# One core: work buffers at multiples of 512 bytes, and three turnings moved to VectorE in squares of 32x32

## The chip, the cores and the metric

The kernel runs on one core of one Trainium2 chip. A core has five engines beside its 16 DMA engines: TensorE for matrix products, VectorE and ScalarE for work on tiles in the on-chip memory (SBUF), GpSimd, and SyncE, which here issues transfers. The metric is the device time of one execution in microseconds; the median of the runs shown is compared. The profile is that of one execution.

## The reference

The reference is one inference step of a two-layer encoder on two requests that share weights: 1024 prompt rows and 32 sample rows of 1024 features, in float32. Cut to what matters:

```python
for i in range(2):
    mod = silu(c) @ w_ada[i] + b_ada[i]                 # c: one vector per request
    sh1, sc1, gt1, sh2, sc2, gt2 = split(mod, 6)
    h = rmsnorm(x, g_norm[i, 0]) * (1 + sc1) + sh1
    if i == 0:    # spatial gating: h @ w_in (1024 -> 4096), gelu, u and v
        v = rmsnorm(v, g_v)
        s = w_s @ v + b_s      # per group, within chunks of 128 rows (sample: 32 rows)
        mix = (u * s) @ w_out  # 2048 -> 1024
    else:         # means over the last 2, 4, 8, 16 rows minus the row, times w_grp
        mix = pool_mixer(h)
    x = x + gt1 * rmsnorm(mix, g_norm[i, 1])
    h = rmsnorm(x, g_norm[i, 2]) * (1 + sc2) + sh2
    f = square(relu(h @ w_up[i])) @ w_down[i]           # 1024 -> 4096 -> 1024
    x = x + gt2 * rmsnorm(f, g_norm[i, 3])
```

The outputs are x of prompt and sample after both layers, and the states of the mixers.

## The kernel before

Activations are kept turned, features on the 128 partitions and rows of x as columns, in three column tiles: 384, 384 and 288 (256 prompt and the 32 sample rows). `acc[t]` holds tile t's x and sums, as 8 blocks of features by 16 columns of halo and the tile's columns. Each large product is three products in float32r, the fast form of float32 on TensorE: value and weight are split into a high and a low part, and high x high (L902), low x high (L903) and high x low (L904) add up in PSUM. `hh`, `hl` are the parts of the normalised input, `fh`, `fl` (and `ush`, `usl`) those of the hidden values. Their names in PSUM are pf (up), pg (down), pu (into the gating mixer), po (out of it); pv is the v half, where the activations stand in the array and 512 columns of weights stream (L929 to L931).

Weights come from memory in pieces of 512 KB. SyncE issues them (`issue`) in the order of one list, `stream`, into three `raw` slots or, for some, into slots of the weight pool itself. `do_w` lets ScalarE make the high part (L417) and VectorE the low part (L79, the helper that every VectorE operation of this kind has as its line); 16 slots "W" hold them. The same list holds the pieces of `w_ada` for the conditioning. `weave` runs between the product groups: it takes steps of the stream while VectorE has room by a running estimate of both engines' time (`time`), and pulls `fillers`, generators for residuals, modulation, pooling and output. `defer` puts a step off by an estimated time. A tile scheduler turns this into one order for each engine.

The conditioning has two forms. The first 16 pieces are products on TensorE with `csil32` (L457); each result is copied by ScalarE, turned by two TensorE transposes (L474) and summed by VectorE. The other slices are multiplied and summed on VectorE into `aa`, 128 partial sums per value. For each slice `fold` puts four products with the matrix `pick` on TensorE (L521), which add over the partitions into four bands of PSUM; ScalarE copies, TensorE turns (L539), and `ada_finish` adds the bias and makes `mod` and `coef`.

In the gating mixer `gate` multiplies v by the spatial weights: psp by chunks of 128 columns (L1211), and for the sample 32 rows by 32 columns (L1219). At the end of layer 1, x of tile 2 ahead of its last residual is turned by 24 TensorE transposes (L1369), copied by ScalarE and sent through memory (`xtd`), and comes back as `xlast` when the last pass starts (`scale_last`, L1342). In that pass the down products of tile 2 are turned as they come (`turn_last`, L1353), their squares are summed over the features by six small products (L1571), and VectorE adds them, scaled, to `xlast`; six transfers write the result (L1599). The outputs of tiles 0 and 1 are fillers (`to_out`): 48 TensorE transposes (L1615), ScalarE copies into a raw slot, six transfers of 512 KB (L1617).

All buffers come from pools that lay them out in the order of allocation. Before the change the pool `work` starts behind constants whose sizes leave its buffers 32 bytes past a multiple of 64; `acc`, `ident` and `ones` lie at multiples of 64.

Of the kernel before, what the change touches and what calls it, by code (L numbers as in the profile page):

```python
# [9 lines left out]
F32 = mybir.dt.float32  # L10
# [5 lines left out]
P = 128  # L16
# [8 lines left out]
NV = 2  # L25
# [9 lines left out]
def tile_stream_encoder_step(  # L35
# [55 lines left out]
    work = pool("work")  # L91
    psum = pool("psum", space=bass.MemoryType.PSUM)
# [8 lines left out]
    hl = [None] * NT  # L101
    acc = [const.tile([P, KB, HALO + n], F32, name=f"acc{t}") for t, n in enumerate(ncol)]
# [4 lines left out]
    xtd = dram.tile([P, len(LAST), D], F32, name="xtd")  # L107
# [9 lines left out]
    pick = const.tile([P, 36], F32, name="pick")  # L117
    nc.vector.memset(pick, 0.0)
    nc.vector.memset(pick[:, 3:4], 1.0)
    inv = const.tile([P, 16], F32, name="inv")  # L120
    epsT = const.tile([P, 1], F32, name="eps")
# [27 lines left out]
    def t_st(name):  # L149
        return work.tile([P, 4], F32, tag="st", bufs=6, name=name)  # L150

    def t_x(name, shape):
        return work.tile(shape, F32, tag="x3", bufs=3, name=name)

    def t_raw(name):
# [3 lines left out]
    rows = [  # L159
        [(g_norm.rearrange("l f (k p) -> (l f k) p", p=P), 64)],  # L160
        [(b_ada.rearrange("l (k p) -> (l k) p", p=P), 96)],
        [
            (c_prompt.rearrange("o (k p) -> (o k) p", p=P), 8),
            (c_sample.rearrange("o (k p) -> (o k) p", p=P), 8),
            (pool_scale.rearrange("o (k p) -> (o k) p", p=P), 8),
            (sgu_g_v.rearrange("o (k p) -> (o k) p", p=P), 16),
        ],
    ]
    vec_rows = [t_m(f"row{i}") for i in range(3)]
    vecs = [  # L170
        const.tile([P, sum(k for _, k in parts)], F32, name=f"vec{i}")
        for i, parts in enumerate(rows)
    ]

# [6 lines left out]
    csil = const.tile([P, KB, NV], F32, name="csil")  # L181
# [30 lines left out]
    ssx = const.tile([P, 9], F32, name="ssx")  # L212
    nc.vector.memset(ssx, 1.0)
    mod = const.tile([P, 2, 48, NV], F32, name="mod")
    coef = const.tile([P, 2, 4, NV, 8], F32, name="coef")
# [213 lines left out]
    def ada_finish(l, sl, view):  # L429

        nk = 2 * view.shape[1]
        m = mod[:, l, 2 * sl : 2 * sl + nk, :].rearrange("p (s h) v -> p s h v", h=2)
        b = bT[:, l * 48 + 2 * sl : l * 48 + 2 * sl + nk].rearrange("p (s h) -> p s h", h=2)
        tt(out=m, in0=view, in1=b.unsqueeze(3).broadcast_to([P, nk // 2, 2, NV]), op=ALU.add)
        which, k0 = sl // 4, 2 * (sl % 4)
        slot = {1: (0, 0), 2: (1, 1), 4: (2, 2), 5: (3, 3)}.get(which)
        if slot is not None:
            cf, gi = slot
            for v in range(NV):
                stt(  # L440
                    out=coef[:, l, cf, v, k0 : k0 + nk],
                    in0=mod[:, l, 2 * sl : 2 * sl + nk, v],
                    scalar=1.0 if cf in (0, 2) else 0.0,
                    in1=g_of(l, gi)[:, k0 : k0 + nk],
                    op0=ALU.add,
                    op1=ALU.mult,
                )


    pe_folds = []  # L450

    def do_ada_pe(l, sl, q, r):
# [16 lines left out]
        act(out=s[:, :256], in_=pa[:, :256], func=AF.Copy)  # L469

        def fold():
            pb = ps_ms(f"adat{l}_{sl}")
            for h in range(2):
                nc.tensor.transpose(pb[:, h * P : (h + 1) * P], s[:, h * P : (h + 1) * P], ident)  # L474
            red = t_st(f"adar{l}_{sl}")
            nc.vector.tensor_reduce(
                out=red.rearrange("p (h m) -> p h m", h=2),
                in_=pb[:, :256].rearrange("p (h c m) -> p h m c", h=2, c=4)[:, :, 0:NV, :],
                op=ALU.add,
# [1189 lines left out]
```

## Time and profile before

| | |
|---|---|
| median of three runs | 2206.67 us (2204.75 to 2207.15) |
| span of the profiled execution | 2201.9 us; its own time is that and some 4.8 us around it, if it stands at the median |
| TensorE busy | 2178.7 us, 99% |
| VectorE busy | 1376.8 us, 63% |
| ScalarE busy | 986.7 us, 45% |
| GpSimd busy | 0.7 us |
| mean granted TensorE clock | 0.999 |
| DMA | 354,976 packets, 312.98 MB, 142 GB/s |

How to read it: the span is the time from the first instruction to the last. PE is TensorE, PEld its weight loads, DVE VectorE, ACT ScalarE, POOL GpSimd, SP SyncE. A row of a group gives line, engine, operation, output and inputs, shape and count, then busy time and mean ns, then idle time ahead of them. A row of the order in time gives start, duration and the instruction; matmuls overlap, so their pace is the distance of the starts and not the duration. A count of records can be twice that of instructions: a float32 product that isn't float32r has two records.

### The profile page before, as it was taken

To read this page: it belongs to the slowest core of one execution; us is meant where nothing else is said; L and a number is where in the kernel's file an instruction comes from. 1 tells how busy PE (TensorE), PEld (TensorE's weight loads), DVE (VectorE), ACT (ScalarE), POOL (GpSimd) and SP (SyncE) were. 2 spreads that over 40 slices of the span, in tenths; PEclk is the share of its full clock that TensorE was granted. 3 is DMA by queue.
4 is the path that set the end of the run, shared out by engine and by line. 5 is a ranking of instruction groups with operands and counts; after the bars stand their busy time and mean duration, and the time that the engine had idled before them with its cause. 6 is when DMAs were issued, how large, how long until landed. Compare 5 with 4: busy or idle time off the path is not lost.

```text
span 2201.9 us, 33431 instructions
## 1 busy us (share of the span) xinstructions
PE 2178.7 (99%) x13383; PEld 2096.0 (95%) x13383; DVE 1376.8 (63%) x2433; ACT 986.7 (45%) x1679; POOL 0.7 (0%) x6
## 2 busy tenths in 40 slices
PE   7999999999999999999999999999999999999998
PEld 5777899999999999999999999999999999999998
DVE  5665746566869556575747879879675553523375
ACT  4633422134447552323445566656564542313354
POOL 0000000000000000000000000000000000000000
PEclk9999999999999999999999999999999999999999
DMA  8475624243527443343645465555454552302343
GB/s 296 128 250 165 201 81 135 89 143 113 154 82 222 148 145 124 102 131 122 191 125 153 149 182 177 180 185 159 139 171 143 155 153 66 107 10 77 97 121 111
DMA packets 354976, 312.98 MB, mean 142 GB/s; under 512 B 10818, under 2 KB 316682, under 8 KB 354820
## 3 DMA queue, kind: packets, MB, share of 16 engines
q1 hardware_dynamic: 352676, 309.43, 45.3%
q8 instruction: 105, 1.72, 0.3%
q10 hardware_dynamic: 2144, 1.41, 0.2%
q14 instruction: 51, 0.42, 0.1%
HBM read 278.95 MB, written 31.84 MB: 141 GB/s over the span
## 4 chain that ended last, share of the span: by engine, by line
PE 96%; DMA 2%; DVE 1%; ACT 1%; SPq 0%; issue 0%; ACTq 0%; DVEq 0%
PE pf L902 12%; PE pf L904 11%; PE pg L902 11%; PE pg L904 11%; PE pg L903 11%; PE pf L903 11%; PE pu L902 3%; PE pu L904 3%; PE po L902 3%; PE po L904 3%; PE po L903 3%; PE pu L903 3%; PE pv L929 2%; PE pv L930 2%; PE pv L931 2%; PE psp L1211 1%
## 5 line engine op out<-in xcount | busy, mean ns | idle before, releaser
L902 PE MATMUL pf<-hh,wh_up 128*128 128x384 f32 (+1 forms) x1536 | 502.6, 327 | 0.0
L902 PE MATMUL pg<-fh,wh_dn 128*128 128x384 f32 (+1 forms) x1536 | 498.0, 324 | 0.0
L904 PE MATMUL pf<-hh,wl_up 128*128 128x384 f32 (+1 forms) x1536 | 496.5, 323 | 0.0
L904 PE MATMUL pg<-fh,wl_dn 128*128 128x384 f32 (+1 forms) x1536 | 494.8, 322 | 0.0
L903 PE MATMUL pg<-fl,wh_dn 128*128 128x384 f32 (+1 forms) x1536 | 494.6, 322 | 0.0
L903 PE MATMUL pf<-hl,wh_up 128*128 128x384 f32 (+1 forms) x1536 | 490.5, 319 | 0.0
L902 PEld LDWEIGHTS pg<-fh,wh_dn 128*128 128x128 f32 x1536 | 288.8, 188 | 4.4 <-issue 3.3
L79 DVE TENSOR_TENSOR wl_up<-raw,wh_up 128x1024 fp32r<-128x1024 f32 x152 | 185.9, 1223 | 167.8 <-ACT wh_up L417 167.8
L902 PEld LDWEIGHTS pf<-hh,wh_up 128*128 128x128 f32 x1536 | 288.2, 188 | 1.3 <-issue 0.8
L903 PEld LDWEIGHTS pg<-fl,wh_dn 128*128 128x128 f32 x1536 | 288.6, 188 | 0.7
L903 PEld LDWEIGHTS pf<-hl,wh_up 128*128 128x128 f32 x1536 | 288.6, 188 | 0.4
L904 PEld LDWEIGHTS pg<-fh,wl_dn 128*128 128x128 f32 x1536 | 288.5, 188 | 0.0
L904 PEld LDWEIGHTS pf<-hh,wl_up 128*128 128x128 f32 x1536 | 287.9, 187 | 0.0
L417 ACT ACTIVATE wh_up<-raw 128x1024 fp32r<-128x1024 f32 x152 | 161.1, 1060 | 278.6 <-PE pf L903 214.3
L79 DVE TENSOR_TENSOR acc<-acc,pg 128x384 f32<-128x384 f32 (+1 forms) x336 | 173.9, 518 | 165.7 <-PE pg L904 164.4
L417 ACT ACTIVATE wh_dn<-raw 128x1024 fp32r<-128x1024 f32 x152 | 161.0, 1060 | 217.7 <-PE pg L903 180.4
L79 DVE TENSOR_TENSOR wl_dn<-raw,wh_dn 128x1024 fp32r<-128x1024 f32 x152 | 185.9, 1223 | 85.3 <-ACT wh_dn L417 85.1
L79 DVE SCALAR_TENSOR_TENSOR aa<-raw,csil,aa 128x512 f32<-128x512 f32 (+1 forms) x364 | 204.3, 621 | 1.9 <-DMA raw<-in_w_ada_dram 1.5
L1293 ACT ACTIVATE r<-pf 128x384 f32<-128x384 f32 (+1 forms) x192 | 86.8, 452 | 197.1 <-PE pf L904 191.7
L79 DVE TENSOR_TENSOR fl<-r,fh 128x384 fp32r<-128x384 f32 (+1 forms) x192 | 100.3, 522 | 104.6 <-ACT fh L1121 103.4
L902 PE MATMUL pu<-hh,wh_u 128*128 128x384 f32 (+1 forms) x384 | 128.0, 333 | 0.0
L902 PE MATMUL po<-ush,wh_o 128*128 128x384 f32 (+1 forms) x384 | 124.2, 324 | 0.0
(264 smaller groups left out, 2899.6 us busy)
## 6 DMA issues: line engine op xcount, KB each, us to landing
raw<-in_ffn_w_up_dram SPq DMA_DIRECT2D x152, 512.0 KB, 4.1
raw<-in_ffn_w_down_dram SPq DMA_DIRECT2D x152, 512.0 KB, 3.4
raw<-in_w_ada_dram SPq DMA_DIRECT2D x96, 512.0 KB, 3.9
raw<-in_sgu_w_in_dram SPq DMA_DIRECT2D x40, 512.0 KB, 4.6
xd<-acc SPq DMA_DIRECT2D x8, 1536.0 KB, 7.4
raw<-in_sgu_w_out_dram SPq DMA_DIRECT2D x24, 512.0 KB, 4.1
xo_r<-xd SPq DMA_DIRECT2D x32, 384.0 KB, 3.3
vd<-vt SPq DMA_DIRECT2D x32, 256.0 KB, 3.3
```

Source lines behind the costliest of these rows:

```text
L79: return op(out, *args, **kw)
L417: act(out=wh, in_=r, func=AF.Copy)
L902: mm(ps[:, :n], wh, rh, start=i == 0, stop=False)
L903: mm(ps[:, :n], wh, rl, start=False, stop=False)
L904: mm(ps[:, :n], wl, rh, start=False, stop=i == last)
L929: mm(ps[:m, :], a_h, wh[:, o : o + 512], start=k == 0, stop=False)
L930: mm(ps[:m, :], a_h, wl[:, o : o + 512], start=False, stop=False)
L931: mm(ps[:m, :], a_l, wh[:, o : o + 512], start=False, stop=k == KB - 1)
L1211: mm(sp[:, c * P : (c + 1) * P], vl[:, c, k * P : (k + 1) * P], wr[:, c * P : (c + 1) * P], start=True, stop=True,)
L1293: act(out=r[:, :n], in_=ps[:, :n], func=AF.Relu)
```

## The change

It has five parts.

1. A new pool `small` takes small tiles and what isn't a multiple of 512 bytes. With the rest reordered, `acc` and every work buffer (`hh`, `hl`, `fh`, `fl`, the weight and raw slots and so on) start at multiples of 512 bytes.
2. The first conditioning results are turned by VectorE in squares of 32x32 straight from PSUM, and `gather`, four small products with `squares` (four unit matrices of 32 on top of one another), adds the bands. It takes the place of a ScalarE copy and two TensorE transposes each.
3. The other slices are turned by VectorE in squares into the raw slot of the last piece and reduced to `sums`; one `gather` for a whole conditioning vector, ten in all, takes the place of 26 folds and 17 transposes. `ada_finish` writes `shift` or `coef` and no longer both.
4. The sample's spatial product has 128 rows: `vl` is zeroed by GpSimd and `wr` by VectorE ahead.
5. The last x of tile 2 goes to memory unturned (four transfers to `xsd`), comes back in nine transfers that order the squares, and is turned by three VectorE transposes at d = 3, 4, 5. The outputs of tiles 0 and 1 are turned by 16 VectorE transposes of 384 columns into `turned` and written by 64 transfers that put the squares in their places, in runs of 128 bytes, 48 issued by SyncE and 16 by GpSimd. In SyncE's order the last piece of weights stands behind the 24 of tile 0, and the six last output transfers behind the 24 of tile 1. In VectorE's order the first of the three transposes of the last x stands before the accumulation of d = 2, the other two behind that of d = 7.

```diff
@@ -89,6 +89,7 @@
 
     const = pool("const")
     work = pool("work")
+    small = pool("small")
     psum = pool("psum", space=bass.MemoryType.PSUM)
     dram = pool("dram", space=bass.MemoryType.DRAM)
 
...
 vecs = [
-        const.tile([P, sum(k for _, k in parts)], F32, name=f"vec{i}")
+        (const if i == 1 else small).tile([P, sum(k for _, k in parts)], F32, name=f"vec{i}")
...
-    xtd = dram.tile([P, len(LAST), D], F32, name="xtd")
+    xsd = dram.tile([DEC, KB, P // DEC, ncol[-1]], F32, name="xsd")
...
-    pick = const.tile([P, 36], F32, name="pick")
-    nc.vector.memset(pick, 0.0)
-    nc.vector.memset(pick[:, 3:4], 1.0)
+    squares = small.tile([P, DEC], F32, name="squares")
+    nc.vector.tensor_tensor(
+        out=squares, in0=ident[:, 0:DEC], in1=ident[:, DEC : 2 * DEC], op=ALU.add
+    )
+    for i in (2, 3):
+        nc.vector.tensor_tensor(
+            out=squares, in0=squares, in1=ident[:, i * DEC : (i + 1) * DEC], op=ALU.add
+        )
...
     def t_st(name):
-        return work.tile([P, 4], F32, tag="st", bufs=6, name=name)
+        return small.tile([P, 4], F32, tag="st", bufs=6, name=name)
     def t_x(name, shape):
-        return work.tile(shape, F32, tag="x3", bufs=3, name=name)
+        return small.tile(shape, F32, tag="x3", bufs=3, name=name)
...
-    mod = const.tile([P, 2, 48, NV], F32, name="mod")
-    coef = const.tile([P, 2, 4, NV, 8], F32, name="coef")
+    shift = small.tile([P, 2, 2, KB, NV], F32, name="shift")
+    coef = small.tile([P, 2, 4, NV, KB], F32, name="coef")
...
@@ -426,26 +431,41 @@
     ada_acc = {}
...
+    def ada_finish(l, which, k0, view):
+
+        nk = view.shape[1]
+        b = bT[:, l * 48 + which * 8 + k0 : l * 48 + which * 8 + k0 + nk]
+        b = b.unsqueeze(2).broadcast_to([P, nk, NV])
+        if which in (0, 3):
+            tt(out=shift[:, l, which // 3, k0 : k0 + nk, :], in0=view, in1=b, op=ALU.add)
+            return
+        cf = {1: 0, 2: 1, 4: 2, 5: 3}[which]
+        c = coef[:, l, cf, :, k0 : k0 + nk]
+        tt(out=c.rearrange("p v k -> p k v"), in0=view, in1=b, op=ALU.add)
+        stt(
+            out=c,
+            in0=c,
+            scalar=1.0 if cf in (0, 2) else 0.0,
+            in1=g_of(l, cf)[:, k0 : k0 + nk].unsqueeze(1).broadcast_to([P, NV, nk]),
+            op0=ALU.add,
+            op1=ALU.mult,
+        )
+
+    def gather(name, parts):
+
+        pa = ps_ms(name)
+        for a, x in enumerate(parts):
+            n = x.shape[1] * x.shape[2]
+            mm(
+                pa[32 * a : 32 * a + 32, :n].rearrange("p (i j) -> p i j", i=x.shape[1]),
+                squares,
+                x,
+                start=True,
+                stop=True,
+                tile_position=(0, 32 * a),
+                skip_group_check=True,
+            )
+        return pa
     pe_folds = []
@@ -466,24 +486,16 @@
         if q == 0:
             return
         s = t_m(f"adas{l}_{sl}")
...
+        nc.vector.transpose(out=s[:, :256], in_=pa[:, :256])
         def fold():
...
+            x = s[:, :256].rearrange("p (h a j) -> p a h j", h=2, a=4)
+            pb = gather(f"adat{l}_{sl}", [x[:, a, :, 0:NV] for a in range(4)])
+            ada_finish(
+                l, sl // 4, 2 * (sl % 4), pb[:, : 2 * NV].rearrange("p (k v) -> p k v", v=NV)
             )
...
         pe_folds.append(fold)
...
     def do_ada(l, sl, q, r, w):
         nq = w // 128
@@ -493,6 +505,7 @@
                 for i in range(nq // 2)
             ]
             ada_acc[0] = [aas[v * nq // 4][:, v * w % 512 :][:, :w] for v in range(NV)]
+            ada_acc["tiles"] = aas
         aa = ada_acc[0]
         for c in range(8 // nq):
             for v in range(NV):
@@ -505,47 +518,32 @@
         if q < nq - 1:
             return
...
+        ns = D // w
+        i = sl % ns
+        which = sl // ns
+        if i == 0:
+            ada_acc["sums"] = small.tile([P, NV, DEC], F32, tag="sums", bufs=2, name=f"sums{l}_{which}")
+        sums = ada_acc["sums"]
+        for j, x in enumerate(ada_acc["tiles"]):
+            time["dve"] += 0.1 + 512 / 930.0
+            nc.vector.transpose(out=r[:, j * 512 : (j + 1) * 512], in_=x)
+        nb = w // DEC
+        time["dve"] += 0.1 + 2 * w / 930.0
+        nc.vector.tensor_reduce(
+            out=sums[:, :, i * nb : (i + 1) * nb],
+            in_=r[:, : 2 * w].rearrange("p (v b j) -> p v b j", v=NV, j=DEC),
+            op=ALU.add,
+            axis=AX.X,
+        )
+        if i < ns - 1:
+            return
+        state["folds"] += 1
         def fold():
...
+            state["folds"] -= 1
+            x = sums.rearrange("p v (k a) -> p a v k", a=4)
+            pa = gather(f"ada{l}_{which}", [x[:, a] for a in range(4)])
+            ada_finish(l, which, 0, pa[:, : NV * KB].rearrange("p (v k) -> p k v", v=NV))
         defer(fold, fold_lag[0])
@@ -633,8 +631,10 @@
     def folds_hold(kind, key):
...
+        if kind not in ("ada", "wide"):
+            return False
+        ns = 4 if kind == "ada" else 2
+        return key[2] == 0 and key[1] % ns == 0 and state["folds"] > 1
     def stream_waits():
...
@@ -1169,6 +1169,7 @@
                 vd[col0 : col0 + npr, g * 256 : (g + 1) * 256].rearrange("(c p) d -> p c d", p=P),
             )
             if nsm:
+                nc.gpsimd.memset(vl[:, nch, :], 0.0)
                 nc.sync.dma_start(
                     vl[:nsm, nch, :], vd[SEQ : SEQ + nsm, g * 256 : (g + 1) * 256]
                 )
@@ -1182,6 +1183,7 @@
                 b = col0 // P + c
                 ts(wr[:, c * P : (c + 1) * P], wt, rv[:, b : b + 1], None, op0=ALU.mult)
             if nsm:
+                nc.vector.memset(wr[:, npr : npr + nsm], 0.0)
                 ts(wr[:nsm, npr : npr + nsm], wt[:nsm, :nsm], rv[:nsm, 8:9], None, op0=ALU.mult)
 
         us = []
@@ -1218,8 +1220,8 @@
                 if nsm:
                     mm(
                         sp[:, npr : npr + nsm],
-                        vl[:nsm, nch, k * P : (k + 1) * P],
-                        wr[:nsm, npr : npr + nsm],
+                        vl[:, nch, k * P : (k + 1) * P],
+                        wr[:, npr : npr + nsm],
                         start=True,
                         stop=True,
                     )
@@ -1335,11 +1337,24 @@
     def scale_last(d):
         t = NT - 1
         if d == 0:
-            last_ps["x"] = room("h", 0, "xlast").rearrange("p k n -> p (k n)").rearrange(
-                "p (b d) -> p b d", d=D
+            last_ps["x"], last_ps["raw"] = (
+                room(part, 0, f"xlast_{part}").rearrange("p k n -> p (k n)").rearrange(
+                    "p (b d) -> p b d", d=D
+                )
+                for part in "hl"
             )
-            for i, (_, r0, nr) in enumerate(LAST):
-                nc.sync.dma_start(last_ps["x"][r0 : r0 + nr, i, :], xtd[r0 : r0 + nr, i, :])
+            src = xsd.rearrange("c k q n -> c (k q) n")
+            for i, (c0, r0, nr) in enumerate(LAST):
+                for r1 in range(r0, r0 + nr, DEC):
+                    nc.sync.dma_start(
+                        last_ps["raw"][r1 : r1 + DEC, i, :].rearrange("p (m n) -> p m n", n=DEC),
+                        src[:, :, c0 + r1 : c0 + r1 + DEC],
+                    )
+        if d in (3, 4, 5):
+            i, r0, nr = d - 3, LAST[d - 3][1], LAST[d - 3][2]
+            nc.vector.transpose(
+                out=last_ps["x"][r0 : r0 + nr, i, :], in_=last_ps["raw"][r0 : r0 + nr, i, :]
+            )
         for c0, w, v in segs[t]:
             a = A(t, d, c0, w)
             act(out=a, in_=a, func=AF.Copy, scale=coef[:, 1, 3, v, d : d + 1])
@@ -1360,20 +1375,8 @@
         need_ada(l, 2)
         yield from residual(st, l, 1, f"r1_{l}_{t}", out)
         if l == 1 and t == NT - 1:
-            yield 0.5
-            for i, (c0, r0, nr) in enumerate(LAST):
-                for half in range(2):
-                    pt = ps_ms(f"xt{i}_{half}")
-                    tick(0.5)
-                    for k in range(4):
-                        nc.tensor.transpose(
-                            pt[:, k * P : (k + 1) * P], A(t, 4 * half + k, c0, P), ident
-                        )
-                    xt = t_x(f"xt{i}_{half}", [P, 512])
-                    act(out=xt[r0 : r0 + nr, :], in_=pt[r0 : r0 + nr, :], func=AF.Copy)
-                    d = slice(half * 512, half * 512 + 512)
-                    nc.sync.dma_start(xtd[r0 : r0 + nr, i, d], xt[r0 : r0 + nr, :])
-                    yield False
+            for q in range(P // DEC):
+                nc.sync.dma_start(xsd[:, :, q, :], acc[t][DEC * q : DEC * (q + 1), :, HALO:])
         need_ada(l, 4)
         yield from modulate(out[0], l, 2, 3)
 
...
@@ -1605,16 +1608,18 @@
                 yield from last()
                 return
             yield from residual(st, 1, 3, f"r2_1_{t}", [], store=False, stat=False)
-            yield 0.5
-            for c0, w, dst in blocks:
-                tick(1.0)
-                yo = t_raw(f"yo{t}_{c0}")
-                for half in range(2):
-                    pt = ps_ms(f"yT{t}_{c0}_{half}")
-                    for i in range(4):
-                        nc.tensor.transpose(pt[:w, i * P : (i + 1) * P], A(t, half * 4 + i, c0, w), ident)
-                    act(out=yo[:w, half * 512 : (half + 1) * 512], in_=pt[:w, :], func=AF.Copy)
-                nc.sync.dma_start(dst, yo[:w, :])
+            turned = room("h", t, f"turned{t}")
+            dst = y_prompt[0, col0 : col0 + npr, :].rearrange(
+                "(b i) (k q c) -> q k i b c", i=DEC, q=P // DEC, c=DEC
+            )
+            for k in range(KB):
+                time["dve"] += 0.1 + npr / 930.0
+                nc.vector.transpose(out=turned[:, k, :], in_=A(t, k))
+                for q in range(P // DEC):
+                    (nc.gpsimd if q == 3 else nc.sync).dma_start(
+                        dst[q, k],
+                        turned[DEC * q : DEC * (q + 1), k, :].rearrange("p (b c) -> p b c", c=DEC),
+                    )
                 yield False
         fillers.append((f"out_{t}", run()))
```

112 lines of the change are left out of this document (23 added, 89 removed).

## The prediction

> **What bounds the kernel now.** I read the page's first and fourth parts first (busy shares, the chain that ended last), then busy time by stretch of the span, then the order of single matmuls in time.
>
> ```profile
> span 2201.9 us, 33431 instructions
> ...
> PE 2178.7 (99%) x13383; PEld 2096.0 (95%) x13383; DVE 1376.8 (63%) x2433; ACT 986.7 (45%) x1679; POOL 0.7 (0%) x6
> ...
> PE 96%; DMA 2%; DVE 1%; ACT 1%; SPq 0%; issue 0%; ACTq 0%; DVEq 0%
> PE pf L902 12%; PE pf L904 11%; PE pg L902 11%; PE pg L904 11%; PE pg L903 11%; PE pf L903 11%; PE pu L902 3%; PE pu L904 3%; PE po L902 3%; PE po L904 3%; PE po L903 3%; PE pu L903 3%; PE pv L929 2%; PE pv L930 2%; PE pv L931 2%; PE psp L1211 1%
> ```
>
> TensorE is on 96% of the chain, nearly all of it the threefold products. So a change pays by what it does to the pace of the matmuls or to their number. The stretches, whose columns are PE, PEld, DVE, ACT, POOL, granted clock, DMA share and GB/s, say where this doesn't hold:
>
> ```profile
> 0.00:60.00 60.00, 46.11 (x301) 32.15 (x301) 33.50 (x105) 30.19 (x57) 0.70 (x6) 1.00 0.84 278
> ...
> 1240.00:1660.00 420.00, 419.54 (x2538) 406.97 (x2537) 329.38 (x543) 257.98 (x441) 0.00 (x0) 1.00 0.56 172
> ...
> 2100.00:2202.00 102.00, 94.15 (x660) 93.14 (x658) 65.95 (x107) 53.18 (x102) 0.00 (x0) 0.97 0.38 124
> ```
>
> In the first 60 us TensorE waits for loads, and at the end there is a tail; elsewhere it is full at full clock. "Busy" doesn't say at which pace. That is read from the starts of successive matmuls (first column; 384, 384, 288 and 512 columns):
>
> ```profile
> 706.06 0.33 PE L903 MATMUL pf<-hl,wh_up 128*128 128x384 f32 x1
> ...
> 707.46 0.34 PE L902 MATMUL pf<-hh,wh_up 128*128 128x384 f32 x1
> ...
> 719.98 0.34 PE L902 MATMUL pg<-fh,wh_dn 128*128 128x384 f32 x1
> ...
> 721.37 0.34 PE L904 MATMUL pg<-fh,wl_dn 128*128 128x384 f32 x1
> ...
> 301.90 0.29 PE L903 MATMUL pu<-hl,wh_u 128*128 128x288 f32 x1
> ...
> 302.83 0.29 PE L904 MATMUL pu<-hh,wl_u 128*128 128x288 f32 x1
> ...
> 211.01 0.40 PE L929 MATMUL pv<-wh_v,hh 128*128 128x512 f32 x1
> ...
> 215.85 0.39 PE L929 MATMUL pv<-wh_v,hh 128*128 128x512 f32 x1
> ```
>
> There are 8, 8, 7 and 21 intervals between these pairs: 175.0, 173.8, 132.9 and 230.5 ns each. What should they be? The products in plain float32 and the transposes are records with more time to each column, and some of them stream buffers that start at multiples of 64 bytes (acc, ident), while all work buffers now lie 32 bytes past such a multiple (from the order and sizes of the allocations):
>
> ```profile
> 1266.57 2.74 PE L1529 MATMUL pp<-acc,wg 128*128 128x384 f32 x8
> ...
> 252.07 1.50 PE L1211 MATMUL psp<-wr,vl 128*128 128x128 f32 x12
> ...
> 2148.80 1.47 PE L1615 MATMUL yT<-ident,acc 128*128 128x128 f32 x12
> ```
> ```profile
> L1211 PE MATMUL psp<-wr,vl 128*128 128x128 f32 x256 | 34.6, 278 | 0.0
> L1529 PE MATMUL pp<-acc,wg 128*128 128x384 f32 x64 | 21.9, 486 | 0.0
> ...
> L1615 PE MATMUL yT<-ident,acc 128*128 128x128 f32 x48 | 6.4, 277 | 0.4 <-ACT yo L1616 0.4
> ```
>
> Taking one mean duration off each row and dividing by the intervals: L1529 (2.74-0.486)/7 = 322 ns, yT (1.47-0.277)/11 = 108.5, psp (1.50-0.278)/11 = 111.1. The two aligned rows give (322-108.5)/256 = 0.834 ns a column and 1.8 fixed; psp, which streams misaligned wr through the same shape as yT, takes 2.6 ns more for 128 columns. The fast form (float32r) needs 173.8/384 = 0.453 ns a column with all its overhead, so its own pace is taken as half of 0.834. With that 384, 288 and 512 columns should take 162, 122 and 215 ns. They take 12.4 (mean of the two), 10.9 and 15.5 more. Per 128 columns that is 3.9 to 4.8 ns, beside the 2.6 of psp: this looks like one cost of reading the moving operand.
>
> **The change part by part.** The sum is made against the profiled execution, its 2201.9 us of span and 4.8 around it, put on the median 2206.7 (the shown runs reach from 2204.8 to 2207.2).
>
> Alignment: every work buffer goes to a multiple of 512 bytes. It adds and removes no instruction. The counts:
>
> ```profile
> L902 PE MATMUL pf<-hh,wh_up 128*128 128x384 f32 x1024 | 351.3, 343 | 0.0
> ...
> L902 PE MATMUL pf<-hh,wh_up 128*128 128x288 f32 x512 | 151.4, 296 | 0.0
> ...
> L902 PE MATMUL pu<-hh,wh_u 128*128 128x384 f32 x256 | 89.4, 349 | 0.0
> ...
> L929 PE MATMUL pv<-wh_v,hh 128*128 128x512 f32 x216 | 86.2, 400 | 0.1
> ```
>
> Three products each for pf, pg (1024) and pu, po (256) are 7680 of 384 columns; half of that, 3840, of 288; some 830 of 512. Full gain: 7680 x 12.4 + 3840 x 10.9 + 830 x 15.5 ns = 95 + 42 + 13 = 150 us. No matmul of the fast form in this trace has an aligned moving operand, so this is bounded: at the good end 150; at the bad end a loss, as pairs of addresses may also clash: pf's 175.0 against pg's 173.8, same shape, other addresses, is 1.2 ns, which would be 14 us over 11,520. I take 144, near the good end, since the psp row shows the misaligned penalty at work, and leave 6 for the first 60 us, where TensorE waits for loads.
>
> Conditioning: 26 folds (14 of 256 columns, 12 of 128) and 17 transposes (L539) go; 10 gathers come. A fold in the stream of matmuls:
>
> ```profile
> 905.07 0.34 PE L904 MATMUL pg<-fh,wl_dn 128*128 128x384 f32 x1
> 905.34 0.64 PE L521 MATMUL ada<-aa,pick 128*32 128x256 f32 x8
> 905.91 0.45 PE L902 MATMUL pg<-fh,wh_dn 128*128 128x384 f32 x1
> 906.20 0.33 PE L903 MATMUL pg<-fl,wh_dn 128*128 128x384 f32 x1
> ```
> ```profile
> L521 PE MATMUL ada<-aa,pick 128*32 128x256 f32 x112 | 8.9, 391 | 0.0
> ...
> L521 PE MATMUL ada<-aa,pick 128*32 128x128 f32 x96 | 5.1, 285 | 0.0
> ```
>
> From 905.07 to 906.20 are two intervals of 0.174 and the fold: 0.78 us, of which its own span is 0.64 (8.9/14). The narrow one spans 5.1/12 = 0.43, with the same edges 0.57. So 14 x 0.78 + 12 x 0.57 + 17 x 0.109 = 19.6 us go. A gather of four tiny matmuls costs at most a narrow fold, at least its edges of 0.14; 0.45, near the top as its edges stay, x10 = 4.5. In the eight first results two transposes give way to one gather each: nothing, within 8 x 0.3 either way. Net -15.
>
> The price is VectorE's. Rows of plain passes:
>
> ```profile
> L79 DVE TENSOR_TENSOR wl_up<-raw,wh_up 128x1024 fp32r<-128x1024 f32 x152 | 185.9, 1223 | 167.8 <-ACT wh_up L417 167.8
> L79 DVE SCALAR_TENSOR_TENSOR aa<-raw,csil,aa 128x512 f32<-128x512 f32 x196 | 135.5, 744 | 1.9 <-DMA raw<-in_w_ada_dram 1.5
> ```
>
> A 512-column transpose or reduction is between 1223/2 = 0.61 and 0.74 us; I take 0.61 for an operation with one input: 12 narrow slices x 1.22 + 14 wide x 2.44 = 49 us over some 1700. It lies beside TensorE, as VectorE is busy 63%; a raw slot is kept those 1.2 or 2.4 us longer, which delays the next weight load on SP's queue, hidden while the 16 W slots hold weights ahead. From 1240 to 1660 VectorE has 329 of 420 busy; with 12 more, in a stretch that shrinks by 8% to 387, it is 88% full. There the cover ends first. I put all new waits (stream steps held back for VectorE, ACT behind it) at +15, between 0 and the 40 by which a stretch of 420 would miss its shortening altogether.
>
> Sample spatial products, padded to 128 rows:
>
> ```profile
> 332.52 0.61 PE L1211 MATMUL psp<-wr,vl 128*128 128x128 f32 x4
> 333.05 0.40 PE L1219 MATMUL psp<-wr,vl 32*128 32x32 f32 x2
> 333.39 0.71 PE L1211 MATMUL psp<-wr,vl 128*128 128x128 f32 x4
> ```
>
> A round takes 0.87; 4 x 0.111 and two short passes of 0.03 would be 0.50. So between 0 and 16 x 0.37 = 5.9; taken at 4, since the round's excess sits at the two changes of row count. The zeroing (eight on GpSimd ahead of loads made early, eight on VectorE) is hidden.
>
> Turned output: 48 yT transposes (1.47/12 = 0.12 each) and 24 xt transposes leave TensorE: -9; 16 passes of 384 columns come to VectorE, by the row above 0.46 each, beside TensorE's last products. 6 + 6 transfers become 64 + 13, in runs of 128 bytes: 24,576 runs out and 9,216 in. The tail:
>
> ```profile
> 2195.16 4.19 DVE L79 SCALAR_TENSOR_TENSOR xlast<-yT,r_last,xlast 128x512 f32<-128x512 f32 x6
> ```
>
> Two more passes of 1024 columns stand there in VectorE's order: 2 x 1.22 = 2.4. What a short run costs isn't in the trace; the nearest is the mean packet of the main queue, and the time left for them starts with the first yT:
>
> ```profile
> q1 hardware_dynamic: 352676, 309.43, 45.3%
> ```
> ```profile
> L1615 PE MATMUL yT<-ident,acc x48: 270/272/329, 2148.8 to 2177.9; 128*128 128x128 f32 x48
> ```
>
> 0.453 x 16 x 2201.9 us / 352,676 = 45 ns for 877 bytes; in proportion to bytes 128 would be 6.6. 33,792 runs over 16 engines are 2112 each: 14 us at the one end, 95 at the other, in 2201.9-2148.8 = 53 us. I take 20 ns, nearer the small end, as most of a packet's time goes with its bytes: 42 us, mostly hidden; +4 for what is still queued at the end. The page "DMA: Bandwidth & Descriptors" of the Trainium skill (Specifications) says that transfers under 512 bytes make the DMA read, modify and write; by that the price would lie nearer 45 than 7, and the sum some 40 us higher. No run here shows it.
>
> Sum: 2206.7 - 144 - 15 - 4 - 9 + 15 + 2.4 + 4 = **2056 us**.
>
> **The rivals.** (a) Address isn't what costs. The fast matmul takes a constant more for each weight load: 162+12, 122+11, 215+15 is not far from one constant of 12. For it: PEld is 95% busy. Against it: the excess grows to 15.5 with 512 columns, and psp has an excess beside yT though both load 128 columns of weights. Then only the removed work counts: 2206.7-15-4-9+6.4+3 = 2188. "TensorE: Matmul & The Clock Gate" of the Trainium skill (Back-to-back issue gap) says just this: that weight load and matmul together set the spacing in a real kernel. Its 131 ns for 512 columns disagrees with the 230.5 of this trace.
>
> (b) Half of it: only some of the reads gain (moving or weights), or VectorE takes the place of TensorE from 1240 to 1660 and gives 40 or more back. 2206.7-72-28+25 = 2132, or 2100 for the second.
>
> (c) Slower: the short runs. At 45 ns they need 95 us of DMA time in a window of 53, and the last weight load stands on SP's queue behind 24 of these transfers, so TensorE would wait for it and VectorE's turns of the last x for their loads. That is +42 at the end. It decides only without the gain of alignment: 2188-4+42 = 2226; from (53+23)/2.112 = 36 ns a run the result is slower. With that gain it would take over 110 ns.
>
> **How the numbers follow.** Under 0.2%, some 4.4 us, this measurement can't tell from no change. Full gain, 0.56: 2056, its own range 2030 to 2100 (waits from 0 to 50, runs from 7 to 36 ns). (b) 0.13, 2100 to 2165. (a) 0.21, 2165 to 2211, of which 0.03 falls within 0.2%. (c) 0.10, 2211 to 2240. Faster 0.87, same 0.03, slower 0.10. From 2030 to 2195 about 8 in 10 are held.
>
> **What would show it.** After the change pg and pf should start every 162 to 164 ns, pv every 216 to 218; at 173 to 175 (a) is true. L521 and L539 should be gone and ten groups of four small matmuls be there; a psp round should take 0.5 us. VectorE's waits from 1240 to 1660 should be by PE, else (b). The turned transfers' time to landing, and what ends VectorE's idle time ahead of the last x, show (c): 3 to 5 us with an end near that of TensorE would be right; tens of microseconds after the last pg would be wrong.

## The result and the profile after

The changed kernel takes 2172.93 us (2170.71 to 2174.44) against 2206.91 (2204.75 to 2207.26): the ratio is 0.9847, with a 95% interval of 0.9833 to 0.9860. It became faster by 34 us. The forecast was faster by 150. The page after, its first and fourth parts:

```profile
span 2171.7 us, 33210 instructions
...
PE 2145.5 (99%) x13214; PEld 2078.1 (96%) x13214; DVE 1431.8 (66%) x2499; ACT 971.3 (45%) x1643; POOL 13.3 (1%) x30
...
PE 93%; DVE 3%; DMA 2%; ACT 1%; issue 1%; ACTq 0%; DVEq 0%; SPq 0%
```

TensorE is still full and still the chain. So the question is its pace. The starts of matmuls after, pg and pf with 384 columns, pv with 512, in the order in time:

```profile
705.96 0.33 PE L902 MATMUL pg<-fh,wh_dn 128*128 128x384 f32 x1
...
708.56 0.33 PE L902 MATMUL pg<-fh,wh_dn 128*128 128x384 f32 x1
...
719.94 0.34 PE L903 MATMUL pf<-hl,wh_up 128*128 128x384 f32 x1
...
721.51 0.33 PE L903 MATMUL pf<-hl,wh_up 128*128 128x384 f32 x1
...
210.80 0.39 PE L929 MATMUL pv<-wh_v,hh 128*128 128x512 f32 x1
...
216.92 0.39 PE L929 MATMUL pv<-wh_v,hh 128*128 128x512 f32 x1
```

Over 15, 9 and 27 intervals that is 173.3, 174.4 and 226.7 ns, where 162, 162 and 215 were forecast and 173.8, 175.0 and 230.5 stood before. Over all matmuls of the traces (intervals more than 15% off the median left out) pf's mean at 384 columns goes from 175.4 to 173.4, pu's from 175.2 to 173.7 and pv's from 231.1 to 228.8; pg and po stay at 173.3 to 173.5. So the places were worth something, but only about 2 ns in some groups: over the counts of pf, pu and pv 6 + 1 + 2 us of the 144.

The removed work went as it should. The start of a round of the sample's spatial product and that of the next, then the new gathers:

```profile
326.03 0.60 PE L1213 MATMUL psp<-wr,vl 128*128 128x128 f32 x4
...
326.62 0.69 PE L1213 MATMUL psp<-wr,vl 128*128 128x128 f32 x4
```
```profile
L459 PE MATMUL ada<-sums,squares 128*32 128x16 f32 x80 | 2.6, 197 | 0.0
...
L459 PE MATMUL adat<-adas,squares 128*32 128x4 f32 x64 | 1.9, 181 | 1.7 <-DVE adas L489 1.7
```

The round takes 0.59 us where it took 0.87 (0.50 forecast): 16 x 0.28 = 4.5 us. VectorE's new work, from its groups:

```profile
L529 DVE STREAM_TRANSPOSE raw<-aa 128x512 f32<-128x512 f32 x40 | 26.7, 695 | 0.1
L532 DVE TENSOR_REDUCE sums<-raw 128x32 f32<-128x1024 f32 x14 | 17.0, 1216 | 0.1
L1617 DVE STREAM_TRANSPOSE turned<-acc 128x384 f32<-128x384 f32 x16 | 8.3, 558 | 0.0
L532 DVE TENSOR_REDUCE sums<-raw 128x16 f32<-128x512 f32 x12 | 8.2, 680 | 0.1
```

That is 51.9 us for the conditioning where 49 were forecast, and no wait of TensorE came of it: in the stretch where VectorE was to be the limit, TensorE (the second number) is busy 399.3 us of 400.

```profile
1240.00:1640.00 400.00, 399.34 (x2422) 387.03 (x2421) 313.40 (x520) 246.61 (x423) 0.00 (x0) 1.00 0.57 172
```

The end, on VectorE, in order of time:

```profile
2159.08 0.45 DVE L79 TENSOR_TENSOR acc<-acc,pg 128x288 f32<-128x288 f32 x1 [0.81 <-PE pg L904]
...
2163.13 1.23 DVE L1355 STREAM_TRANSPOSE xlast_h<-xlast_l 128x1024 f32<-128x1024 f32 x1
2164.40 1.41 DVE L79 SCALAR_TENSOR_TENSOR xlast_h<-yT,r_last,xlast_h 128x512 f32<-128x512 f32 x2
2165.84 1.24 DVE L1355 STREAM_TRANSPOSE xlast_h<-xlast_l 32x1024 f32<-32x1024 f32 x1
```

From the last accumulation (2159.08) to the end of the span it takes 12.6 us, where it took 9.5 (2192.43 to 2201.9): +3.1, of which 2.5 are the two turns. Of the transfers:

```profile
q1 hardware_dynamic: 380452, 308.64, 46.8%
```

The main queue has 27,776 packets more and 0.468 x 16 x 2171.7 - 0.453 x 16 x 2201.9 = 302 us more of engine time. These are differences, in which the longer packets of the old outputs are gone. The trace's own packets say what a short run costs: 27,648 of 128 bytes on this queue took 12.6 ns each on the mean, 348 us in all, or 22 us for each of the 16 engines; a packet of 512 bytes took 28.3. The share of the outputs that GpSimd issues went out on a queue of its own as 256 packets of 3072 bytes. So the short runs cost 12.6 of the 20 ns taken, far from the 36 that rival (c) needed: the turned outputs landed in a median of 3.0 us, the last outputs in 2.0 where they took 2.1 before, and TensorE shows no wait from 2100 us on.

| term | forecast, us | measured, us |
|---|---|---|
| places of the buffers | -144 | -9 |
| conditioning | -15 | -12 |
| sample's product | -4 | -5 |
| outputs and last x, with the tail | -3 | -5 |
| new waits | +15 | none |

The second column is measured one part at a time, in the runs that follow.

### The profile page after: what moved, and what is told of

Its sections match the earlier page's. It is cut to its first block, busy times and chain, and to the rows that moved or that the text cites. A ratio compares the mean times of both kernels' runs of the same rounds, so it can differ in the third digit from the quotient of the medians.

```text
span 2171.7 us, 33210 instructions
## 1 busy us (share of the span) xinstructions
PE 2145.5 (99%) x13214; PEld 2078.1 (96%) x13214; DVE 1431.8 (66%) x2499; ACT 971.3 (45%) x1643; POOL 13.3 (1%) x30
## 4 chain that ended last, share of the span: by engine, by line
PE 93%; DVE 3%; DMA 2%; ACT 1%; issue 1%; ACTq 0%; DVEq 0%; SPq 0%
PE pg L902 11%; PE pg L903 11%; PE pg L904 11%; PE pf L902 11%; PE pf L904 11%; PE pf L903 11%; PE po L902 3%; PE po L903 3%; PE po L904 3%; PE pu L902 3%; PE pu L904 3%; PE pu L903 3%; PE pv L929 2%; PE pv L930 2%; PE pv L931 2%; PE pp L1532 1%
## 5 line engine op out<-in xcount | busy, mean ns | idle before, releaser
L902 PE MATMUL pf<-hh,wh_up 128*128 128x384 f32 (+1 forms) x1536 | 494.4, 322 | 0.0
```

The lines of the kernel that those rows point to most:

```text
L902: mm(ps[:, :n], wh, rh, start=i == 0, stop=False)
```

## The experiments

From pg and pv after the change, (226.7 - 173.3) / 128 = 0.417 ns is the price of a column, and 173.3 - 384 x 0.417 = 13 ns, some 32 columns' worth, is left. A cycle below is the time of one such column. The theories: A, each float32r matmul costs a constant of 32 cycles more than its columns, whatever the address; what the new places gained is something smaller. B, the excess is a clash between streams or between stream and weights, which equal places only moved. C, the constant is the load of the weights.

**The matmul by itself.** Rows of 32 matmuls of each form, nothing else, in one execution:

```python
    for name, kind, cols, rows, n, om, ow in forms:
        ...
            nc.tensor.matmul(ps[:cols, :n], lhs, rhs, start=i == 0, stop=i == N_EACH - 1)
```

> The computation is left out: this kernel runs only rows of 32 matmuls, one form after another, and writes zeros. It measures the disputed cost by itself: the distance of the starts at 384 columns, which stood at 173.5 ns in the changed kernel with every buffer at a multiple of 512 bytes, where 162 were forecast. Theory A, a constant of 32 cycles of 0.417 ns on each float32r matmul, whatever the address: 173.3 ns with the streamed operand or the weights 0, 32 or 64 bytes past the multiple, 66.7, 120, 133.3 and 226.7 ns at 128, 256, 288 and 512 columns, 162 for bfloat16. Theory B, a clash of two equal phases (weights and streamed operand now both at 0): 173 at equal phases and about 162 where only one of them is shifted. Theory C, the constant is the load of 128 columns of weights: 166.7 ns with 64 columns, 163.3 with 32, against 173.3 in all three by theory A alone; the same weights each time change nothing in any of them unless the load is skipped.

The order in time, each row some matmuls from the middle of one form; in this order: all at 0; streamed operand 32 past; 64 past; weights 32 past; streamed operand 32 and weights 96 past; 128, 256, 288 and 512 columns; 64 and 32 columns of weights; bfloat16. Below them the groups, for the mean of one.

```profile
15.79 4.52 PE L115 MATMUL ps_a<-mv,wt 128*128 128x384 f32 x25
21.70 3.63 PE L115 MATMUL ps_m<-mv,wt 128*128 128x384 f32 x20
26.73 4.50 PE L115 MATMUL ps_m<-mv,wt 128*128 128x384 f32 x25
32.81 3.98 PE L115 MATMUL ps_w<-mv,wt 128*128 128x384 f32 x22
38.19 4.00 PE L115 MATMUL ps_mw<-mv,wt 128*128 128x384 f32 x22
...
43.36 2.84 PE L115 MATMUL ps_n<-mv,wt 128*128 128x128 f32 x24
47.13 3.04 PE L115 MATMUL ps_n<-mv,wt 128*128 128x256 f32 x24
50.75 3.46 PE L115 MATMUL ps_n<-mv,wt 128*128 128x288 f32 x25
55.40 5.39 PE L115 MATMUL ps_n<-mv,wt 128*128 128x512 f32 x23
62.68 3.63 PE L115 MATMUL ps_c<-mv,wt 128*64 128x384 f32 x20
68.75 3.46 PE L115 MATMUL ps_c<-mv,wt 128*32 128x384 f32 x19
87.71 3.58 PE L115 MATMUL ps_b<-mb,wb 128*128 128x384 bf16 x21
```
```profile
L115 PE MATMUL ps_f384m<-mv,wt 128*128 128x384 f32 x64 | 20.8, 486 | 0.0
L115 PE MATMUL ps_f<-mv,wt 128*128 128x384 f32 x64 | 20.8, 486 | 0.0
L115 PE MATMUL ps_m<-mv,wt 128*128 128x384 f32 x64 | 11.3, 337 | 0.0
...
L115 PE MATMUL ps_b<-mb,wb 128*128 128x384 bf16 x32 | 5.4, 326 | 0.0
```

The granted clock is 1.00 in all these rows. One mean duration off, over the intervals: 174.3, 173.3, 173.5, 173.5 and 174.4 ns for the five places. The 174.3 comes from the row's first starts, which are still uneven; from its eighth on they are 173.3 apart. The last keeps up some 174.7 to its end. So no single place gains anything, and B, by which the rows with one operand shifted were to take 162, falls. With 256, 288 and 512 columns (means of 285, 294 and 390 ns) it is 119.8, 131.9 and 227.3: columns and 32 cycles give 120, 133.3 and 226.7, so 288 is 1.4 below the rule. With 64 and 32 columns of weights it stays at 173.4 and 173.5 where 166.7 and 163.3 were C's, and rows with the same weights each time and with 64 rows settle at 173.3 too: C falls at 384 columns. At 128 columns (273 ns) it is 111.6 where 66.7 were expected: a miss of A, taken up below. In bfloat16 it is (3.58-0.326)/20 = 162.7, just the pace that the prediction took for "its own". And plain float32 goes at the same pace with its operand at 0 and 32 bytes past (the two ps_f groups), so it could have shown nothing of addresses either.

**The new places alone.** Two places of its edit; the rest orders the constants and moves other small tiles in the same way.

```diff
     work = pool("work")
+    small = pool("small")
...
-    pick = const.tile([P, 36], F32, name="pick")
+    pick = small.tile([P, 36], F32, name="pick")
```

> The kernel before with the new places of the buffers alone. By the starts of the changed kernel, pf goes from 175.8 to 173.5 ns, pv from 232 to 227 and psp from 111.8 to 109.5, which over their counts is 7 + 2 + 0.6 us: theory A expects 2197 us (-10). The theory of the prediction expected 2063. If places matter to other engines or to DMA too, it would fall below 2190.

2197.22 us (2196.44 to 2198.33), ratio 0.9957 (0.9944 to 0.9971): 9 us, as A had it.

**All buffers 96 bytes on.**

```diff
     onesr = const.tile([P, P], F32R, name="ones")
+    gap = const.tile([P, 24], F32, name="gap")
+    nc.vector.memset(gap, 0.0)
```

> The changed kernel with every work buffer moved by 96 bytes, so that all lie 32 past a multiple of 64, at equal phase. If the phase against 64 bytes is what costs pf its 2.3 ns, pf and pg go to 175 to 176 ns and the time to about 2182 us (+9). If it was the difference of phases between buffers (352 against 32 and 416 before), nothing changes: 173.5 ns and 2173.

2173.32 us (2170.05 to 2174.47), against 2172.93: nothing. Being at a multiple of 512, or of 64, isn't what counts. What is left is how the places stand to one another.

**Which step between places.** Rows of 36 with two streams in the order of a product, first, second, first:

```python
            second = i % 3 == 1
            at = (o1 if second else o0) // 4
```

> The computation is left out: rows of 36 matmuls of float32r, in the order first stream, second stream, first stream. If what the new places gained is the step between two streams that start at different places within 512 bytes, the pair 352 and 32 with the weights at 352, which is the kernel before, gives 175.8 ns on the mean at 384 columns, and 352 twice 173.3; 0 and 192, the same step, gives 175.8 too. If it is 352 with the weights at 352, both of the first give 175.8 and 0 and 192 give 173.3. At 160, 192 and 224 columns: 80, 93.3 and 106.7 ns if the constant of 32 cycles holds there; the first of these runs had 111.6 ns at 128 columns, where 66.7 were expected, so a floor between 107 and 112 may show. If the floor at 128 columns is the load of the weights, it falls with 64 and 32 columns of weights; if not it stays at 111.

The order in time: streams at 352 and 32 with the weights at 352, which is pf before; both at 352; at 0 and 192 with the weights at 0; at 192 and 0, the same with the order exchanged; then 160 columns, and 128 with 64 and 32 columns of weights. The groups below.

```profile
15.72 4.55 PE L106 MATMUL ps_phase352x<-mv,wt 128*128 128x384 f32 x25
22.74 4.50 PE L106 MATMUL ps_phase352x<-mv,wt 128*128 128x384 f32 x25
28.82 4.38 PE L106 MATMUL ps_phase0x<-mv,wt 128*128 128x384 f32 x24
35.31 3.98 PE L106 MATMUL ps_phase192x<-mv,wt 128*128 128x384 f32 x22
...
53.68 2.51 PE L106 MATMUL ps_wide<-mv,wt 128*128 128x160 f32 x21
...
69.44 1.78 PE L106 MATMUL ps_few<-mv,wt 128*64 128x128 f32 x27
71.59 1.61 PE L106 MATMUL ps_few<-mv,wt 128*32 128x128 f32 x24
```
```profile
L106 PE MATMUL ps_phase352x<-mv,wt 128*128 128x384 f32 x72 | 12.7, 336 | 0.0
...
L106 PE MATMUL ps_wide<-mv,wt 128*128 128x160 f32 x36 | 4.1, 275 | 0.0
...
L106 PE MATMUL ps_few<-mv,wt 128*32 128x128 f32 x36 | 2.3, 224 | 0.0
```

352 and 32 give 175.6 ns, 352 twice 173.5, 0 and 192 175.8. So the places of before, put side by side, cost what pf lost, and equal ones don't; that is what the new places bought in pf. But it isn't the step from one stream's place to the next one's alone: 192 and 0, which makes the same steps with the order exchanged, gives 173.6 (mean of 335 ns), and the rows of 0 with 64 and of 0 with 256 settle at 174.0 and 173.3. In the first of these runs the row with the streams 32 and the weights 96 past lost 1.4 ns without any step. Which combinations cost stays open, and those of pu and pv were not tried in rows. At 160 columns it is 111.8 and not the 80 expected, the rows of 192 and 224 have the same 111.7, and so has 128. With 64 columns of weights and 128 streamed it falls to 59.9, and stays at 60.3 with 32. So there is a floor, 112 ns for 128 columns of weights, which hangs on the columns of weights; above it the constant, which doesn't.

**The conditioning, the outputs and the sample, each with the new places.** Each is one part of the change on top of the new places, the other parts left as before. The core of each edit:

```diff
-        act(out=s[:, :256], in_=pa[:, :256], func=AF.Copy)
+        nc.vector.transpose(out=s[:, :256], in_=pa[:, :256])
...
+        for j, x in enumerate(ada_acc["tiles"]):
+            nc.vector.transpose(out=r[:, j * 512 : (j + 1) * 512], in_=x)
```

> New places and the turned conditioning sums and first results, without the changes of the outputs, the last x and the sample's products. From the starts of TensorE's instructions the conditioning is worth 12 us there (12.3 of L521, 2.1 of waits around it, 1.0 of L539, 4.0 of L474 less 5.2 of gathers and some 2 around): 2185 us if all of it stays on the path. If VectorE, with 49 us more, is late in return, 2190 or more.

2185.13 us (2182.27 to 2187.54), 12.1 below the new places alone: all of it stays on the path.

```diff
-                        nc.tensor.transpose(pt[:w, i * P : (i + 1) * P], A(t, half * 4 + i, c0, w), ident)
...
+                nc.vector.transpose(out=turned[:, k, :], in_=A(t, k))
```

> New places and the turned outputs and last x, with the conditioning and the sample's products as before. Against the new places alone (2197.2 us) TensorE loses 8.1 us (5.4 of L1615, 2.7 of L1369) and the tail behind the last product grows by 3, as in the changed kernel (9.5 to 12.6 us): 2192. If the short runs held anything up, 2197 or more; if VectorE's extra turns cost nothing at the end, 2189.

2192.70 us (2190.89 to 2194.27), 4.5 below.

```diff
-                        vl[:nsm, nch, k * P : (k + 1) * P],
-                        wr[:nsm, npr : npr + nsm],
+                        vl[:, nch, k * P : (k + 1) * P],
+                        wr[:, npr : npr + nsm],
```

> New places and the padded sample products alone. By the starts in the changed kernel the 32 short products go from 5.3 to 2.3 us: 2194, 3 below the new places alone. If the change of row count cost nothing, 2197.

2192.60 us (2191.42 to 2196.17), 4.6 below. The four parts sum to 9 + 12.1 + 4.5 + 4.6 = 30, against 34 together; each has an interval of some 3 us either way, and whether the 4 are more than that stays open. Taken against the runs of before beside them, whose medians were 2206.2 for the first two and 2207.4 for the last two, the last two come to 5.7 and 5.8, and the sum to 33.

**The pace that was forecast.** The parts in bfloat16; the arithmetic changes and is less exact:

```diff
-        wh = work.tile([P, 1024], F32R, tag="W", bufs=W_SLOTS, name="wh_" + "_".join(map(str, key)))
-        wl = work.tile([P, 1024], F32R, tag="W", bufs=W_SLOTS, name="wl_" + "_".join(map(str, key)))
+        wh = work.tile([P, 1024], F32, tag="W", bufs=W_SLOTS, name="wh_" + "_".join(map(str, key)))
+        wl = work.tile([P, 1024], F32, tag="W", bufs=W_SLOTS, name="wl_" + "_".join(map(str, key)))
+        wh, wl = (x.bitcast(BF16)[:, :1024] for x in (wh, wl))
...
-        hh[t] = room("h", t, f"hh{l}_{cf}_{t}", F32R)
+        hh[t] = room("h", t, f"hh{l}_{cf}_{t}").bitcast(BF16)[:, :, : ncol[t]]
```

> The changed kernel with the high and low parts in bfloat16 instead of float32r, which makes the result less exact; instructions, order and counts stay. It gives the large products the pace that the prediction took for them (162, 122 and 216 ns measured apart). Theory A, the constant goes with the form float32r: 135 us less on TensorE (85 at 384, 38 at 288, 11 at 512 columns), so 2038 us if nothing else is late, 2053 with the prediction's 15 us of new waits, and the stretch from 1240 would show VectorE as releaser. If VectorE or ScalarE is the bound close behind, 2080 or more.

2059.31 us (2053.96 to 2060.94), ratio 0.9327 (0.9314 to 0.9339). The starts, and the stretches:

```profile
699.77 0.33 PE L904 MATMUL pg<-fh,wh_dn 128*128 128x384 bf16 x1
...
701.39 0.33 PE L905 MATMUL pg<-fl,wh_dn 128*128 128x384 bf16 x1
```
```profile
60.00:560.00 500.00, 489.81 (x2998) 296.50 (x3011) 352.78 (x747) 191.70 (x339) 2.29 (x7) 0.99 0.51 156
560.00:1200.00 640.00, 634.21 (x4143) 406.29 (x4142) 466.86 (x737) 307.14 (x504) 0.31 (x1) 1.00 0.50 152
1200.00:1560.00 360.00, 355.54 (x2327) 233.43 (x2326) 299.90 (x504) 233.94 (x407) 0.00 (x0) 1.00 0.61 182
```

Ten intervals of 162 ns. Of the 135 us that the pace frees, 114 come out. The rest is waits: TensorE's idle time in the whole span goes from 26.2 to 45.9 us. They are spread: it idles 10.2, 5.8 and 4.5 us in these three stretches, against 2.5, 0.5 and 0.7 in the changed kernel's. The stretch from 1200 us, where VectorE was to be late, isn't where most of them lie. So the forecast's sum (2056) comes within 3 us for a kernel that has the pace, in part by luck, as its other terms erred both ways; and the change didn't give the pace.

**The same on the kernel before**, to see whether places matter to bfloat16. The edit is the one above.

> The kernel before, places and all, with the parts in bfloat16 (less exact). If the form alone sets the pace, the starts are 162.5 ns apart at 384 columns though no buffer is at a multiple of 64 bytes, and the time is that of the changed kernel in bfloat16 and the removed work of conditioning, sample and outputs, 2059.3 + 24 = 2083 us. If places matter to bfloat16 as the prediction had it, 2100 or more.

2082.35 us (2081.81 to 2085.04), ratio 0.9436 (0.9422 to 0.9450). In its order in time:

```profile
699.88 0.33 PE L904 MATMUL pf<-hh,wh_up 128*128 128x384 bf16 x1
...
701.34 0.33 PE L904 MATMUL pf<-hh,wh_up 128*128 128x384 bf16 x1
```

Nine intervals of 162 ns, as in the changed kernel, though no work buffer starts at a multiple of 64. It is the form that sets this pace; the places did nothing to it in these two kernels.

**The tail.**

```diff
-                    (nc.gpsimd if q == 3 else nc.sync).dma_start(
+                    (nc.gpsimd if q >= 2 else nc.sync).dma_start(
```

> The changed kernel with half of the 64 output transfers issued by GpSimd instead of a quarter. SyncE's order then has room for the loads of the last x, and in VectorE's order the three turns of the last x stand ahead of the last accumulations. If the two turns behind the last product are what lengthens the tail, it goes from 12.6 to about 10 us and the time to 2170.5; if the transfers were, it stays at 2173 or grows with GpSimd's issue.

2168.91 us (2168.08 to 2169.71), ratio 0.9827 (0.9813 to 0.9840). VectorE's order now:

```profile
2156.30 1.24 DVE L1355 STREAM_TRANSPOSE xlast_h<-xlast_l 32x1024 f32<-32x1024 f32 x1
2157.58 0.45 DVE L79 TENSOR_TENSOR acc<-acc,pg 128x288 f32<-128x288 f32 x1
...
2160.29 4.19 DVE L79 SCALAR_TENSOR_TENSOR xlast_h<-yT,r_last,xlast_h 128x512 f32<-128x512 f32 x6
```

From 2157.58 to the end of its span (2167.3) it is 9.7 us: the tail of before is back. That is 2.9 of the 4.4 us between the two spans; the last accumulation also came 1.5 earlier. More transfers on GpSimd did no harm. With parts in float32r this is the fastest of these kernels.

**Both.** The parts in bfloat16 and the edit of the tail together, on the changed kernel.

> The changed kernel with the parts in bfloat16 (less exact) and half of the output transfers issued by GpSimd. The two gains touch different stretches, so they add: 2059.3 - 4 = 2055 us.

2058.18 us (2056.21 to 2060.30), ratio 0.9327 (0.9312 to 0.9343). That is 1 below and not 4, within what the runs can tell; the tail is shorter by 2.4 us in the traces (2044.20 to 2054.4, against 2043.60 to 2056.2), and the last accumulation came 0.6 later.

## Why the prediction was wrong

The direction was right; the size wasn't: 34 us where 150 were forecast, and what failed is one step. The prediction took the pace of float32r as half of the 0.834 ns a column of plain float32, with the same small fixed part, and called all the rest a cost of reading a misaligned operand. The constant belongs to the form float32r: 173.5 - 162.7 = 10.8 ns over the pace of bfloat16 at 384 columns, 227.3 - 215.9 = 11.4 at 512 (both forms in the rows by themselves), and 131.9 - 122.5 = 9.4 at 288 (the 122.5 from the kernel in bfloat16). What in float32r makes it stays open. The term "alignment", put at 144 us, measured 9. No row of before could show the aligned case, as the prediction itself said; it bridged that with rows of another form (L1529 and yT), whose pace doesn't show the constant.

The numbers for the right reading stood in the prediction. The three excesses were 12.4, 10.9 and 15.5 ns at 384, 288 and 512 columns. Taken as one constant with a remainder, the constant is at most the smallest, 10.9, and the remainders 1.5, 0 and 4.6 ns are all that a place could have caused: 7680 x 1.5 + 830 x 4.6 ns = 15 us, where 9 were measured. Instead the growth to 15.5 was used to throw out the constant as a whole, in rival (a). And pf's 175.0 against pg's 173.8, a pair of one shape at different places, was used as a bound for a loss only; it was a measurement of what places are worth.

The psp row was the other support. Its 2.6 ns over yT is worth 256 x 2.6 ns = 0.7 us; but it was taken as the sign of the large term, when it had the size of the small one. And it wasn't the place at all. In the changed kernel wr starts at a multiple of 512, and the row is what it was:

```profile
246.72 1.50 PE L1213 MATMUL psp<-wr,vl 128*128 128x128 f32 x12
```

With its mean of 277 ns that is (1.50 - 0.277) / 11 = 111.2 ns, where 111.1 stood before. psp is a product and yT a transpose; the 2.6 ns lie between these, whatever their cause.

Rival (a), with 0.21, was nearest: 2188 against 2172.9. It is right in the constant; it erred in giving the places nothing, in charging 3 us of waits, and in a tail of 6.4 where 3.1 came. Its cause, the weight load, is wrong at 384 columns: with a quarter of the columns of weights the pace stayed at 173.5. What the Trainium skill says in "TensorE: Matmul & The Clock Gate" (Back-to-back issue gap), that the load and the matmul set the spacing together, is seen here only in the floor of 112 ns below 256 columns. The gap of N / 2.4 + 2.5 ns, which the same section of the Trainium skill gives for a matmul by itself, is 162.5 at 384 columns and agrees with the 162.7 of bfloat16, here in a row with a load for each matmul, and not with the 173.3 of float32r.

The other steps held. Conditioning -12 for -15: a gather takes 0.40 us between wide matmuls where 0.45 were taken, but the first results gained nothing and TensorE waited 1.7 us for VectorE there (the row of adat). Sample -5 for -4. Outputs and last x -5 for -3, since short runs cost 12.6 ns and not 20, and nothing was queued at the end: the last outputs landed as fast as before. The two turns behind the last product cost 2.5 for 2.4. The new waits of 15 us didn't come, because the pace that would have made VectorE late didn't; where it was given, TensorE idled some 20 more. Rival (c) had a bound of 36 ns a run for going slower; at 12.6, 2112 runs take 27 us of an engine in a window of 53. Its second bound, 110 ns with the gain of alignment, comes out as (53 + 2211 - 2052) / 2.112 = 100 from its own terms, which changes nothing.

## What to carry to other kernels

An excess over an ideal pace has to be split before it is given to a cause: what is the same in every shape is a constant, and only what differs between equal shapes at different places can be the place. An ideal pace must come from the same form of instruction; where the trace has none, a row of thirty such instructions on the chip costs little beside a term that carries most of a forecast. A supporting row is worth testing in the same way: psp kept its excess when its place changed. In float32r with three products, wide columns and few matmuls pay, since each matmul has its 10 ns or so beside bfloat16's pace; bfloat16 parts, where their accuracy is enough, paid 114 us here, the places 9.

## What the runs showed of the hardware that was not expected

- A float32r matmul starts every (columns + 32) x 0.417 ns from 256 columns on (119.8, 173.5 and 227.3 ns at 256, 384 and 512; 131.9 at 288 is 1.4 below), with 128, 64 or 32 columns of weights; bfloat16 of the same shape has 162.7 at 384. Eight choices of places at 384 columns, of operands and of two streams, settled at 173.3 to 174.0 ns.
- Below that stands a floor of 112 ns (128 to 224 columns) with 128 columns of weights, and of 60 (128 columns streamed) with 64 or 32.
- Some combinations of places within 512 bytes cost 1 to 2 ns a matmul on the mean: 175.6 for streams at 352 and 32, as much for 0 and 192, and some 174.7 for streams at 32 with weights at 96. The same two places in the other order, 192 and 0, cost nothing (173.6), nor did equal ones at 352 (173.5). No rule for it was found.
- A packet of 128 bytes took the DMA engines 12.6 ns, one of 512 bytes 28.3: 1.8 times as much for a byte. The read, modify and write that the Trainium skill's "DMA: Bandwidth & Descriptors" (Specifications) states for transfers under 512 bytes can't be told apart in this; if it has a price, it lies within these 12.6 ns.
